# A hybrid streaming-encoder layer: packed token columns for the state-space inputs, moved memory rates, and another order at the end of the MLP's up-projection

## The chip, the cores and the metric

One core of a Trainium2 chip runs the whole program. The metric is the device time of one execution in microseconds (us), over several runs of the same program on the same chip.

## The reference

One residual layer over 1024 tokens of 1024 channels, in three sub-layers, each normalised before and after. All arrays are float32.

```python
def reference(x, mem, ...):
    h = rms_norm(x, norm_mix_pre)
    q, k, v, u, gate_logits = jnp.split(h @ w_in, splits, axis=-1)      # 512 columns each for q, k, v, u; 2048 for the gates
    gate_attn, gate_ssm = jnp.split(jax.nn.sigmoid(gate_logits + b_gate), 2, axis=-1)
    o_attn = stick_breaking_attention(q, k, v)                          # 8 heads of 64
    o_ssm = s5_branch(u, ...)                                           # 32 groups of 16 channels, 64 complex states each
    merged = gate_attn * (o_attn @ w_branch_attn) + gate_ssm * (o_ssm @ w_branch_ssm)
    x = x + rms_norm(merged @ w_out, norm_mix_post)
    h = rms_norm(x, norm_xa_pre)
    mem_n = rms_norm(mem, norm_mem)                                     # 256 memory rows
    x = x + rms_norm(memory_cross_attention(h, mem_n, ...), norm_xa_post)
    h = rms_norm(x, norm_ffn_pre)
    f = conv_ffn(h, w_up, conv_w, conv_b, w_down)
    return x + rms_norm(f, norm_ffn_post)

def conv_ffn(h, w_up, conv_w, conv_b, w_down):
    up = h @ w_up                                # 1024 -> 2 * 2816
    up = conv1d(up, conv_w, causal, width 3, per channel) + conv_b
    gate, val = jnp.split(up, 2, axis=-1)
    return (jax.nn.gelu(gate) * val) @ w_down    # 2816 -> 1024
```

## The kernel before

**Numbers in two halves.** Each float32 operand of a matmul is split into a high part (a copy into the type fp32r) and a low part (the difference), and each product is three matmuls: high by high, high by low, low by high (`mm3`, L148 to L151, of which the last three lines are the matmuls). The high parts are mostly made by ScalarE and the low parts by VectorE.

**The first part: input projection.** `hT` holds x transposed, in four tiles: high and low part of channel blocks 0 to 3 and of 4 to 7; in each, the 1024 tokens lie side by side. A step `tokens(now, n, i, k)` is the three matmuls of one block of 128 channels for one tile of 128 tokens, the tokens as weights and 512 columns of the projection streaming. For n = 0 the result is the attention's V, and the tile is 128 consecutive tokens. For n = 1 it is u, the state-space branch's input; tile i holds the tokens i, i+8, i+16 and so on (`slice(i, S, 8)`), since the scan that follows works with eight interleaved streams. After the eighth step of a tile ScalarE evicts it: V into `vr` and on to DRAM, scaled by each token's rate (L447), u into `U`, scaled by `r8` (L444). The normalisation is thus applied behind the projection. `r8` holds the rates in the interleaved order: they are written to DRAM (`rx_d`, L413) and read back (L414) on SP's queue of DMAs. Squares of x (for the rates) come from x loaded as rows, in a ring of two buffers named `xr` (pool `p0`).

The raw float32 weights of the projection arrive in a ring of four buffers named `wr`; w_high (L393, ScalarE) and w_low (L397, VectorE) make the pairs `wh`/`wl` (`wx` for the last pair). The same ring takes the 256 memory rows later (`mem_load`), whose rates `mem_rate` makes: a Square on ScalarE, a scaled sum on VectorE, a power on POOL.

All of this is ordered by hand. `at(t, go)` puts a step into a heap at a planned time t, and the steps are issued in the order of these times; a step of TensorE is planned at 0.70 (`STEP`), and `line(t, ...)` places a list of steps at and after t. PE, ACT, DVE and POOL keep that order (a manual schedule), and so does SP's queue. While the u tiles run, VectorE builds the state-space tables (L660 and around, with two tables' cosines on ScalarE), and 16 narrow matmuls (L694, `W` with `Y`) stand between u steps. The first gate job (`ps_f`, L149 to L151) follows the last u tile.

**The MLP's up-projection.** The pair of blocks p = 0 to 21 (`NF` = 22) is 128 gate channels and 128 value channels. A seven-product block scheme makes both for all 1024 tokens from 7 products of 12 matmuls instead of 8. `order` lists (pair, product); `prep` makes the weights' operand some products ahead; `product` issues the 12 matmuls and then drains the bank: a copy on ScalarE (L1927) where the bank is the first into its place in `uu`, an addition on VectorE (L1932) otherwise. Products of one pair share banks: 1, 6, 7 and 4 accumulate into one, 5 and 3 into another, 2 has its own. `chores` places the convolution of the pair before among the products: `c_scale` on ScalarE (L2023), two `c_tap` on VectorE (L2027) for each half (1 is the value half, `cv`; 0 the gate half, `cg`), then `c_gelu` and the gating product `c_mul` (L2035). The gated halves and their sums go to DRAM as `sd`; those of the weights as `td`.

**The down-projection** is a second seven-product scheme: `load2` reads an operand pair back as `raw`, `prep2` splits it into `dn` (L154 on ScalarE, L155 on VectorE), and `mm_step` issues 12 matmuls (L2177 to L2179) into four banks, four token tiles in turn. Its first products take the operands of pairs that were done long before; the last pair's are wanted by the eleventh step. The banks of the accumulators change hands at its door: a bank of the down-projection opens once the up-projection's product in it has been drained. In the MLP a scheduler orders ACT and DVE, from the order of the code and its own estimates.

**The tail.** The last product of the scheme goes token tile by token tile. ScalarE squares the finished half row (L2256), VectorE multiplies it by the gain (L2257), `rstd_of` makes the row's rate (L213, L214, and a power on POOL), and a scaled addition and a DMA end the row.

Of the kernel before, what the change touches and what calls it, by code (L numbers as in the profile page):

```python
# [45 lines left out]
def kernel(ctx: ExitStack, tc: tile.TileContext, a: dict, out: bass.AP, dbg=None):  # L46
# [382 lines left out]
    accs_ = {}  # L429

    def tokens(now, n, i, k):

        sl = slice(i * P, (i + 1) * P) if n == 0 else slice(i, S, 8)
# [4 lines left out]
        mm3(acc, h_hi(k, sl), h_lo(k, sl), wh, wl, k == 0, k == KT - 1)  # L438
# [60 lines left out]
    def mem_load(i):  # L499
        raw["m", i] = px.tile([P, 1024], F32, tag="wr", name="wr", bufs=4)  # L500
        dma(raw["m", i], a["mem"][i * P:(i + 1) * P, :])
# [10 lines left out]
    line(70.0, (lambda: mem_load(0), 0), (lambda: mem_load(1), 16.0), (lambda: mem_rate(0), 1.4), (lambda: mem_rate(1), 2.6),  # L512
# [307 lines left out]
    u_begin = clock  # L820
    for c in range(4):
        at(30.0 + c, lambda _, c=c: w_load(1, c))
        at(last_v + 1.3 + 1.4 * c, lambda _, c=c: w_high(1, c))
        at(last_v + 2.4 + 1.4 * c, lambda _, c=c: w_low(1, c))
# [977 lines left out]
    class Pair:  # L1802
# [46 lines left out]
        def operand(self, prod):  # L1849
# [12 lines left out]
            if prod == 5:  # L1862
                src = self.add("1", self.wv[:, lo_], self.wg[:, lo_])
            elif prod == 6:
                src = self.add("2", self.wv[:, hi_], self.t["1"])
# [15 lines left out]
    order[-7:] = [(NF - 1, 1), (NF - 2, 4)] + [(NF - 1, n) for n in (5, 6, 2, 7, 3, 4)]  # L1881
# [193 lines left out]
    def chores(w, r):  # L2075
# [10 lines left out]
        slot = r - 2 if p == 0 else r  # L2086
        if live and slot == 0:
            c_scale(p, 1)
        elif live and slot == 1:
            c_tap(p, 1, 1)  # L2090
        elif live and slot == 2:
            c_tap(p, 1, 2)
            c_scale(p, 0)
        elif live and slot == 3:
            c_tap(p, 0, 1)
        elif live and slot == 4:
            c_tap(p, 0, 2)
# [51 lines left out]
    for s in range(last + 1):  # L2149
# [6 lines left out]
        if s == 9:  # L2156
            down_load(0)
        chores(w, r)
        product(*order[s])
        if s >= last - 4:  # L2160
            for _ in range(3 if s == last - 4 else 1):
                load2()
        if s in (last - 3, last - 2):
            prep2()
# [16 lines left out]
    def out_row(i, t, ss, two):  # L2181
# [3 lines left out]
        rr = rstd_of(p8, ss, two=two)  # L2185
        yt = y[t // 4][:, i]
# [18 lines left out]
    for prod in (2, 1, 5, 6, 3, 7):  # L2205
        acc = bank_b if prod in (2, 5, 3) else bank_a
        for k in range(NF // 2):
# [11 lines left out]
            elif i2 == 4:  # L2219
                chores(NF + 1, 4)  # L2220
                r7.close()
# [23 lines left out]
    for i in range(4):  # L2245
# [11 lines left out]
        V.tensor_tensor(y[1][:, i, h0], bank_a[i], gfo[:, h0], op=ALU.mult)  # L2257
        out_row(i, 4 + i, ss1[i], True)
# [71 lines left out]
```

## Time and profile before

| what | before |
|---|---|
| runs | 1667.44, 1664.74, 1667.44 us; median 1667.44 |
| the profiled execution | 1663.46 us, its span 1661.7 us |
| granted TensorE clock | 0.997 |
| TensorE matmuls / weight loads | 1642.4 us (99%) / 1382.1 us (83%) |
| VectorE, ScalarE, POOL | 1163.4 us (70%), 881.7 us (53%), 199.3 us (12%) |
| HBM | 163 GB/s over the span |

The span is what the profiler saw from the first to the last instruction; the execution's own time is 1.8 us more. The span divides as follows on TensorE's timeline: V tiles to 54.24 us, u tiles from there to 104.23, then gates, attention, cross-attention, and the MLP, whose up-projection issues its last matmul at 1443.16 and whose down-projection begins at 1445.09.

A row of the timeline reads: start in us, duration in us, engine, line, operation, output<-inputs, shapes, and in brackets how long the engine had idled and for whom. Matmuls are pipelined, so that their starts are closer together than they are long: what counts is the distance of the starts. A group's row has the count, then busy time in us and the mean of one in ns, then the idle time before it and what ended it.

### The profile page before, as it was taken

The page shows a single profiled execution, that of the slowest core. Times are in us where ns is not written, and L with a number is a line of the kernel's source. Part 1 is how long each engine was busy: PE and PEld are TensorE (multiplying, and loading weights), DVE is VectorE, ACT ScalarE, POOL GpSimd, SP SyncE. Part 2 cuts the span into 40 slices and gives each one's busy share as a digit, 9 for nine tenths or more (in the row PEclk, how much of TensorE's full clock was granted, in tenths as well). Part 3 has the DMA queues.
Part 4 walks back from the last instruction along what each step waited for, and adds up shares of the span by engine and source line. Part 5 has one row for each costly group of instructions (what it writes and reads, how often), then busy time and mean ns, then how long its engine had stood idle before and what let it go on. Part 6 is the DMA issues. An engine that isn't in the chain of part 4 may idle for free.

```text
span 1661.7 us, 22448 instructions
## 1 busy us (share of the span) xinstructions
PE 1642.4 (99%) x8126; PEld 1382.1 (83%) x8126; DVE 1163.4 (70%) x1617; ACT 881.7 (53%) x1458; POOL 199.3 (12%) x233
## 2 busy tenths in 40 slices
PE   9999999999999999999999999999999999999998
PEld 7998888888888978888888888888888888788886
DVE  7778637676866678467655678888887788965473
ACT  5435346676766554345444556655565555654441
POOL 5000002233332000011000000111111111000010
PEclk9999999999999999999999999999999999999999
DMA  9412244232432964464313584677777676697672
GB/s 324 121 46 66 67 141 110 65 90 86 109 108 92 341 208 135 161 205 164 140 64 135 192 285 176 179 212 211 216 197 202 185 201 189 204 350 235 194 234 83
DMA packets 125438, 279.26 MB, mean 168 GB/s; under 512 B 23696, under 2 KB 28304, under 8 KB 125200
## 3 DMA queue, kind: packets, MB, share of 16 engines
q1 hardware_dynamic: 113664, 251.35, 46.0%
q0 software_dynamic: 9360, 18.09, 6.2%
q10 hardware_dynamic: 2304, 8.39, 1.3%
q8 instruction: 64, 1.05, 0.3%
q14 instruction: 46, 0.38, 0.1%
HBM read 203.98 MB, written 67.38 MB: 163 GB/s over the span
## 4 chain that ended last, share of the span: by engine, by line
PE 90%; DVE 5%; DMA 2%; ACT 1%; issue 1%; SPq 0%; DVEq 0%; POOL 0%; POOLq 0%; ACTq 0%
PE ps_p L1916 8%; PE ps_p L1914 8%; PE ps_p L1915 8%; PE ps_f L149 7%; PE ps_f L151 6%; PE ps_f L150 6%; PE ps_d L2177 4%; PE ps_d L2178 4%; PE ps_d L2179 4%; PE ps_m L149 3%; PE ps_m L151 3%; PE ps_m L150 3%; PE ps_o L1065 2%; PE ps_w L1040 2%; PE ps_z L149 1%; PE ps_z L151 1%
## 5 line engine op out<-in xcount | busy, mean ns | idle before, releaser
L149 PE MATMUL ps_f<-hT,wh 128*128 128x512 f32 x384 | 165.4, 431 | 0.0
L151 PE MATMUL ps_f<-hT,wl 128*128 128x512 f32 x384 | 150.9, 393 | 0.0
L150 PE MATMUL ps_f<-hT,wh 128*128 128x512 f32 x384 | 150.6, 392 | 0.0
L1915 PE MATMUL ps_p<-qS,bm 128*128 128x512 f32 (+2 forms) x368 | 141.3, 384 | 1.7 <-DVE qS L1741 1.7
L1914 PE MATMUL ps_p<-qS,bm 128*128 128x512 f32 (+2 forms) x368 | 141.3, 384 | 0.6 <-DVE uu L1932 0.6
L1916 PE MATMUL ps_p<-qS,bm 128*128 128x512 f32 (+2 forms) x368 | 141.4, 384 | 0.0
L155 DVE TENSOR_TENSOR dn<-raw,dn 128x1024 fp32r<-128x1024 f32 x77 | 93.4, 1222 | 66.5 <-ACT dn L154 63.2
L1020 DVE TENSOR_TENSOR_SCAN s<-s,zcol 128x128 f32<-128x128 f32 (+3 forms) x96 | 99.4, 1037 | 50.5 <-ACT s L1015 49.9
L154 ACT CAST dn<-raw 128x1024 fp32r<-128x1024 f32 x77 | 80.6, 1054 | 92.1 <-PE ps_d L2179 38.7
L2177 PE MATMUL ps_d<-dn 128*128 128x512 f32 x308 | 119.9, 389 | 1.5 <-ACT uu L1927 1.5
L1026 POOL TENSOR_TENSOR s<-s,s 128x127 f32<-128x127 f32 (+4 forms) x96 | 89.3, 931 | 256.1 <-DVE s L1020 222.3
L2179 PE MATMUL ps_d<-dn 128*128 128x512 f32 x308 | 119.8, 389 | 0.0
L2178 PE MATMUL ps_d<-dn 128*128 128x512 f32 x308 | 119.8, 389 | 0.0
L1916 PE MATMUL ps_p<-qA,bm 128*128 128x512 f32 (+2 forms) x272 | 105.0, 386 | 0.5 <-DVE bm L1847 0.5
L1914 PE MATMUL ps_p<-qA,bm 128*128 128x512 f32 (+2 forms) x272 | 105.1, 386 | 0.0
L1915 PE MATMUL ps_p<-qA,bm 128*128 128x512 f32 (+2 forms) x272 | 105.0, 386 | 0.0
L1927 ACT COPY uu<-ps_p 128x512 f32<-128x512 f32 (+2 forms) x90 | 51.5, 572 | 83.8 <-PE ps_p L1916 83.8
L1859 POOL DMA_DIRECT2D bm<-in_ffn_up_T x61 | 52.8, 866 | 354.4 <-ACT bm L1858 161.0
L1015 ACT ACTIVATE s<-ps_z,rates_x 128x128 f32<-128x128 f32 (+3 forms) x96 | 56.3, 587 | 57.7 <-PE ps_z L1007 29.1
L151 PEld LDWEIGHTS ps_f<-hT,wl 128*128 128x128 f32 x384 | 72.1, 188 | 16.1
L1915 PEld LDWEIGHTS ps_p<-qS,bm 128*128 128x128 f32 x368 | 70.1, 190 | 15.1 <-DVE qS L1741 2.0
L1914 PEld LDWEIGHTS ps_p<-qS,bm 128*128 128x128 f32 x368 | 70.0, 190 | 14.2 <-issue 1.2
(545 smaller groups left out, 4446.6 us busy)
## 6 DMA issues: line engine op xcount, KB each, us to landing
raw<-sd SPq DMA_DIRECT2D x77, 256.0 KB, 3.3
bm<-in_ffn_up_T POOLq DMA_DIRECT2D x61, 256.0 KB, 5.5
ws<-in_w_in_T SPq DMA_DIRECT2D x24, 512.0 KB, 3.3
ws<-in_xa_wo_N SPq DMA_DIRECT2D x23, 512.0 KB, 4.1
wv<-in_ffn_up_T SPq DMA_DIRECT2D x22, 512.0 KB, 4.3
wg<-in_ffn_up_T SPq DMA_DIRECT2D x22, 512.0 KB, 4.1
dr<-in_ffn_down SPq DMA_DIRECT2D x22, 512.0 KB, 6.7
td<-st SPq DMA_DIRECT2D x44, 256.0 KB, 6.4
```

The costliest lines, as they stand in the source:

```text
L149: T.matmul(acc, sh, mh, start=first, stop=False)
L150: T.matmul(acc, sh, ml, start=False, stop=False)
L151: T.matmul(acc, sl, mh, start=False, stop=last)
L155: (lo or V).tensor_tensor(dl, src, f(dh), op=ALU.subtract)
L1020: V.tensor_tensor_scan(s2[:, n0:n1][:, ::-1], s2[:, n0:n1][:, ::-1], zcol.to_broadcast([P, n1 - n0]), 1.0 if diag else s2[:, n1:n1 + 1], o ...
L1026: G.tensor_tensor(s1[:, n0:e], s1[:, n0:e], s2[:, n0 + 1:e + 1], op=ALU.mult)
L1914: T.matmul(acc, bm[:, 0, ks], q[:, 0, k, cs], start=alone and k == 0, stop=False, skip_group_check=True)
L1915: T.matmul(acc, bm[:, 0, ks], q[:, 1, k, cs], start=False, stop=False, skip_group_check=True)
L1916: T.matmul(acc, bm[:, 1, ks], q[:, 0, k, cs], start=False, stop=k == 3, skip_group_check=True)
L2177: T.matmul(acc[i], v[:, 0, 0, sl], v[:, 0, 1], start=first, stop=False, skip_group_check=True)
L2178: T.matmul(acc[i], v[:, 0, 0, sl], v[:, 1, 1], start=False, stop=False, skip_group_check=True)
L2179: T.matmul(acc[i], v[:, 1, 0, sl], v[:, 0, 1], start=False, stop=last, skip_group_check=True)
```

## The change

**Packed columns for u.** For each of the eight u tiles, four new copies on ScalarE (`every_eighth`) put the tile's tokens side by side: from each tile of `hT` the columns i, i+8 and so on of four channel blocks, 128x512 at a time, into a buffer `uc`. The two `uc` of a tile (high and low) stand in the ring `wr` of four. The u steps then take their weights from `uc`. The copies are planned 4.2 ahead of their tile and 1.1 apart; those of the first tile 1.3 ahead and 0.6 apart.

**Memory rows and rates.** Since `wr` now holds `uc`, the two memory rows' tiles go into `xr`, the ring of the rows of x. Their loads and rates move from the planned time 70.0 to 47.5.

**End of the up-projection.** The last pair's products come in the order 6, 5, 7, 2, 4, 3 instead of 5, 6, 2, 7, 3, 4, with the operand code to suit. The last pair's gate half is convolved before its value half. In the last five steps the product now stands ahead of the chores, and the first two `prep2` one step later. From the fifth step from the end to the fifth step of the down-projection ScalarE keeps the order of the code (`seam`).

**Tail.** The gain of the last four rows is handed to `out_row` and issued behind the call of `rstd_of`.

```diff
+    def every_eighth(i, j, kk):
+        if kk == 0:
+            ucol.setdefault(i, []).append(px.tile([P, 1024], F32R, tag="wr", name="uc", bufs=4))
+        C.copy(ucol[i][j][:, kk * 512:(kk + 1) * 512].rearrange("p (k t) -> p k t", k=4), hT[j][kk][:, :, i::8])
     def tokens(now, n, i, k):
-        sl = slice(i * P, (i + 1) * P) if n == 0 else slice(i, S, 8)
+        sl = slice(i * P, (i + 1) * P)
...
-        mm3(acc, h_hi(k, sl), h_lo(k, sl), wh, wl, k == 0, k == KT - 1)
+        stat = [c[:, k * P:(k + 1) * P] for c in ucol[i]] if n else (h_hi(k, sl), h_lo(k, sl))
+        mm3(acc, *stat, wh, wl, k == 0, k == KT - 1)
...
     def mem_load(i):
-        raw["m", i] = px.tile([P, 1024], F32, tag="wr", name="wr", bufs=4)
+        raw["m", i] = p0.tile([P, D], F32, tag="xr", name="xr", bufs=2)
...
-    line(70.0, (lambda: mem_load(0), 0), (lambda: mem_load(1), 16.0), (lambda: mem_rate(0), 1.4), (lambda: mem_rate(1), 2.6),
+    line(47.5, (lambda: mem_load(0), 0), (lambda: mem_load(1), 14.0), (lambda: mem_rate(0), 1.4), (lambda: mem_rate(1), 2.6),
...
+    for i in range(8):
+        for n, (j, kk) in enumerate(((0, 0), (1, 0), (0, 1), (1, 1))):
+            t_ = u_begin + 8 * STEP * i - 4.2 + 1.1 * n if i else u_begin - 1.3 + 0.6 * n
+            at(t_, lambda _, i=i, j=j, kk=kk: every_eighth(i, j, kk))
...
-    order[-7:] = [(NF - 1, 1), (NF - 2, 4)] + [(NF - 1, n) for n in (5, 6, 2, 7, 3, 4)]
+    order[-7:] = [(NF - 1, 1), (NF - 2, 4)] + [(NF - 1, n) for n in (6, 5, 7, 2, 4, 3)]
...
+        one = int(p < NF - 1)
         if live and slot == 0:
-            c_scale(p, 1)
+            c_scale(p, one)
...
-        chores(w, r)
+        if s < last - 4:
+            chores(w, r)
+            product(*order[s])
+            continue
+        if s == last - 4:
+            seam = ExitStack()
+            seam.enter_context(tc.manual_schedule(engines={mybir.EngineType.Activation}))
         product(*order[s])
-        if s >= last - 4:
-            for _ in range(3 if s == last - 4 else 1):
-                load2()
-        if s in (last - 3, last - 2):
+        chores(w, r)
+        for _ in range(3 if s == last - 4 else 1):
+            load2()
+        if s in (last - 2, last - 1):
             prep2()
...
             elif i2 == 4:
                 chores(NF + 1, 4)
+                seam.close()
...
-        V.tensor_tensor(y[1][:, i, h0], bank_a[i], gfo[:, h0], op=ALU.mult)
-        out_row(i, 4 + i, ss1[i], True)
+        out_row(i, 4 + i, ss1[i], True,
+                lambda: V.tensor_tensor(y[1][:, i, h0], bank_a[i], gfo[:, h0], op=ALU.mult))
```

How the instructions stand on an engine's own queue, at three places. In these rows a line number is that of the kernel named; behind the name is the operation, output<-inputs and the shape.

**ScalarE, from the last weights of the projection on.** `wr` are raw weights, `wh` and `wx` their high parts, `vr` evictions of V, `U` of u, `uc` the packed columns, `mss` the memory rows' sums of squares. Before:

```order
L393 CAST wh_646<-wr_478 128x1024
L393 CAST wx_656<-wr_489 128x1024
L447 ACTIVATE vr_667<-ps_m_554,zcol_109,rates_x_119 128x512
L444 ACTIVATE U_148<-ps_m_659,zcol_109,r8_153 128x32x16
L447 ACTIVATE vr_701<-ps_m_605,zcol_109,rates_x_119 128x512
L444 ACTIVATE U_148<-ps_m_688,zcol_109,r8_153 128x32x16
```

Changed:

```order
L435 COPY uc_680<-hT01_127 128x512
L435 COPY uc_688<-hT11_129 128x512
L451 ACTIVATE U_148<-ps_m_668,zcol_109,r8_153 128x32x16
L435 COPY uc_717<-hT00_126 128x512
L454 ACTIVATE vr_719<-ps_m_605,zcol_109,rates_x_119 128x512
L435 COPY uc_733<-hT10_128 128x512
L512 ACTIVATE xr_616,mss_738<-xr_616 128x1024
L435 COPY uc_717<-hT01_127 128x512
L435 COPY uc_733<-hT11_129 128x512
L512 ACTIVATE xr_618,mss_764<-xr_618 128x1024
```

The copies stand ahead of the casts `wx` and between the evictions, and the two memory Squares now stand there too.

**SP's queue of DMAs, around the rates of x.** `rx_d` as an output is the write of the rates, `r8` their load back, `ws` weights for later stages, `v_d` V on its way to DRAM, `row_k` another reader of the rates, `wr<-in_mem` and `xr<-in_mem` the memory rows. Before:

```order
L259 DMA ws_916<-in_w_in_T 128x1024
L259 DMA ws_964<-in_w_in_T 128x1024
L413 DMA rx_d_122<-rates_x_119 128x8x1
L448 DMA v_d_66<-vr_622 128x512
L414 DMA r8_153<-rx_d_122 128x8
L287 DMA row_k_121<-rx_d_122 128x512
L501 DMA wr_784<-in_mem 128x1024
L501 DMA wr_786<-in_mem 128x1024
```

Changed:

```order
L508 DMA xr_616<-in_mem 128x1024
L508 DMA xr_618<-in_mem 128x1024
L413 DMA rx_d_122<-rates_x_119 128x8x1
L259 DMA ws_964<-in_w_in_T 128x1024
L455 DMA v_d_66<-vr_626 128x512
L414 DMA r8_153<-rx_d_122 128x8
L287 DMA row_k_121<-rx_d_122 128x512
L259 DMA ws_1012<-in_w_in_T 128x1024
```

The memory loads moved from behind the load of `r8` to just ahead of the write of the rates, in the place of a load of later weights (`ws`).

**ScalarE at the end of the up-projection.** `uu<-ps_p` is the drain of a product, `cv` and `cg` the convolution's scales of the value and gate half, `dn` the casts for the down-projection. Before:

```order
L154 CAST dn_13051<-raw_13034 128x1024
L2023 ACTIVATE cv_13013<-uu_9482,cw_9746 128x1024
L1927 COPY uu_9482<-ps_p_12870 128x4x128
L154 CAST dn_13051<-raw_13055 128x1024
L2023 ACTIVATE cg_13067<-uu_9482,cw_9746 128x1024
```

Changed:

```order
L1940 COPY uu_9530<-ps_p_12918 128x4x128
L154 CAST dn_13041<-raw_12991 128x1024
L2036 ACTIVATE cg_13076<-uu_9530,cw_9794 128x1024
L154 CAST dn_13099<-raw_12994 128x1024
L154 CAST dn_13099<-raw_13020 128x1024
L2036 ACTIVATE cv_13117<-uu_9530,cw_9794 128x1024
```

The last drain that is ScalarE's (product 4, now the last but one) stands ahead of the convolution's first scale, which is now that of the gate half.

More of the change, by code (lines that the diff above doesn't have):

```diff
@@ L427, in x_low @@
         V.tensor_tensor(dl, xt[t][:, 4 * kk:4 * kk + 4], f(dh), op=ALU.subtract)
-    accs_ = {}
+    accs_, ucol = {}, {}
+    def every_eighth(i, j, kk):
+        if kk == 0:
+            ucol.setdefault(i, []).append(px.tile([P, 1024], F32R, tag="wr", name="uc", bufs=4))
+        C.copy(ucol[i][j][:, kk * 512:(kk + 1) * 512].rearrange("p (k t) -> p k t", k=4), hT[j][kk][:, :, i::8])
     def tokens(now, n, i, k):
-        sl = slice(i * P, (i + 1) * P) if n == 0 else slice(i, S, 8)
+        sl = slice(i * P, (i + 1) * P)
         if k == 0:
@@ L1862, in operand @@
             if prod == 5:
-                src = self.add("1", self.wv[:, lo_], self.wg[:, lo_])
+                src = self.t["1"] if "1" in self.t else self.add("1", self.wv[:, lo_], self.wg[:, lo_])
             elif prod == 6:
+                if "1" not in self.t:
+                    self.add("1", self.wv[:, lo_], self.wg[:, lo_])
                 src = self.add("2", self.wv[:, hi_], self.t["1"])
@@ L2086, in chores @@
         slot = r - 2 if p == 0 else r
+        one = int(p < NF - 1)
         if live and slot == 0:
-            c_scale(p, 1)
+            c_scale(p, one)
         elif live and slot == 1:
-            c_tap(p, 1, 1)
+            c_tap(p, one, 1)
         elif live and slot == 2:
-            c_tap(p, 1, 2)
-            c_scale(p, 0)
+            c_tap(p, one, 2)
+            c_scale(p, 1 - one)
         elif live and slot == 3:
-            c_tap(p, 0, 1)
+            c_tap(p, 1 - one, 1)
         elif live and slot == 4:
-            c_tap(p, 0, 2)
+            c_tap(p, 1 - one, 2)
         if live and p and slot == 5:
@@ L2157 @@
             down_load(0)
-        chores(w, r)
-        product(*order[s])
-        if s >= last - 4:
-            for _ in range(3 if s == last - 4 else 1):
-                load2()
-        if s in (last - 3, last - 2):
+        if s < last - 4:
[5 more added lines that the diff above has]
+            seam.enter_context(tc.manual_schedule(engines={mybir.EngineType.Activation}))
+        product(*order[s])
+        chores(w, r)
+        for _ in range(3 if s == last - 4 else 1):
+            load2()
+        if s in (last - 2, last - 1):
             prep2()
@@ L2179, in mm_step, with out_row @@
             T.matmul(acc[i], v[:, 1, 0, sl], v[:, 0, 1], start=False, stop=last, skip_group_check=True)
-    def out_row(i, t, ss, two):
+    def out_row(i, t, ss, two, gain=lambda: None):
         xt = p8.tile([P, D], F32, tag="x2t", name="x2t", bufs=3)
@@ L2185, in out_row @@
         rr = rstd_of(p8, ss, two=two)
+        gain()
         yt = y[t // 4][:, i]
```

## The prediction

> **What bounds the kernel now.** I read the page first, then TensorE's waits, then the timelines of the places that the diff touches.
>
> ```profile
> PE 1642.4 (99%) x8126; PEld 1382.1 (83%) x8126; DVE 1163.4 (70%) x1617; ACT 881.7 (53%) x1458; POOL 199.3 (12%) x233
> PE 90%; DVE 5%; DMA 2%; ACT 1%; issue 1%; SPq 0%; DVEq 0%; POOL 0%; POOLq 0%; ACTq 0%
> ...
> PE ps_d L2177 <- ACT uu L1927: 1.5, 1, 1.5
> ```
>
> TensorE is busy for 99% of the span and is 90% of the chain that ended last. Time can only be won by matmuls that follow each other faster, or by one of TensorE's few waits going away. The third line is the longest wait that the diff touches: at the door of the down-projection.
>
> ```profile
> 43.18 0.39 PE L149 MATMUL ps_m<-wh,hT 128*128 128x512 f32 x1
> ...
> 54.24 0.41 PE L149 MATMUL ps_m<-wh,hT 128*128 128x512 f32 x1
> ...
> 76.94 1.85 PE L694 MATMUL ps_m<-Y,W 128*128 128x16 f32 x16
> ...
> 104.23 0.39 PE L149 MATMUL ps_f<-hT,wh 128*128 128x512 f32 x1
> ...
> 106.95 0.49 PE L723 MATMUL ps_m<-ident,U 128*128 128x128 f32 x3
> ```
>
> These are starts on TensorE's timeline. 43.18 to 54.24 are the last two V tiles, 48 matmuls: 0.2304 us each. At 54.24 the u tiles begin; up to the small W matmuls at 76.94 they are 31 steps of 3, 93 matmuls: 0.2441 us each. At 104.23 the first gate job begins, 12 matmuls to 106.95: 0.2267 us each. Only the u tiles take every eighth column as weights, and their weight loads show it (groups of loads in 59 to 104 us, then in 7 to 59):
>
> ```profile
> L150 PEld LDWEIGHTS ps_m<-wl,hT 128*128 128x128 f32 x42 | 13.9, 331 | 0.0
> ...
> L150 PEld LDWEIGHTS ps_m<-wl,hT 128*128 128x128 f32 x54 | 11.0, 203 | 2.7 <-DVE wl L467 0.5
> ```
>
> A load of 331 ns no longer fits under a matmul of 0.23 us.
>
> **Part 1, packed weights.** 64 steps of 3 are 192 matmuls. They gain 192 x (0.2441 - 0.2304) = 2.6 us by their neighbours before, 192 x (0.2441 - 0.2267) = 3.3 us by those after; I take 3.0.
>
> What it costs is 32 copies of 128x512 on ScalarE, four ahead of each u tile. No row has ScalarE reading every eighth float, so the bounds come from these:
>
> ```profile
> L423 ACT CAST hT<-xt 128x512 fp32r<-128x512 f32 x16 | 9.6, 616 | 15.4 <-DVE xt L420 15.4
> L793 ACT COPY U<-ps_m 128x512 f32<-128x512 f32 x8 | 8.9, 1222 | 3.6 <-PE ps_m L791 3.6
> ...
> L596 DVE TENSOR_TENSOR t<-sp x1: 189/189/189, 43.8 to 43.8; 128x32 f32<-128x32 f32 x1
> ...
> L600 DVE TENSOR_TENSOR t<-pi,sp x1: 203/203/203, 44.6 to 44.6; 128x32 f32<-128x32 f32 x1
> ```
>
> Below: 0.62 us, a cast between packed tiles. Above: 1.22 us, L793, which writes every eighth float. Between: L600 reads one operand at 36 bytes' distance (pi[:, :, 1]) and takes 14 ns longer for 32 elements than L596, 0.44 ns an element, over 512 elements 0.22 us. I take 0.62 + 0.22 = 0.84 us, since L600 is a strided read by an elementwise engine, as the copy is; both ends are kept. On ScalarE an instruction starts about 0.1 us before the one ahead ends, so a copy adds 0.74 us to its queue.
>
> The Trainium skill (page "SBUF — State Buffer", section "Door 1: The DMA port swizzle") speaks against the copies: it says SBUF is read in lines of 16 bytes and that every access which crosses to a new line pays, so four floats is the widest free stride. At eight floats each element is a new line, which would put the copies near the upper row and the sum at that of the first rival below; the weight loads (331 against 203 ns) agree with it, L600 only by a third.
>
> **The first u tile waits.** The copies' buffers are the four that hold the raw weights of this projection, so a copy waits until VectorE has made the low part of a weight.
>
> ```profile
> 51.69 2.17 ACT L393 CAST wh<-wr 128x1024 fp32r<-128x1024 f32 x2
> 54.44 1.05 ACT L393 CAST wx<-wr 128x1024 fp32r<-128x1024 f32 x1 [0.58 <-PE ps_m L151]
> ...
> 52.74 3.49 DVE L397 TENSOR_TENSOR wl<-wr,wh 128x1024 fp32r<-128x1024 f32 x3
> ```
>
> The three low parts end at about 53.9, 55.1 and 56.2. High columns, first half: 53.9 to 54.75, so the first matmul comes at 54.8 and not at 54.24 (0.55 late). Low columns: 55.1 to 55.95, so the third matmul comes at 56.0 and not at 55.25 (0.75 late). The cast wx and the second halves then end near 58.3, when step 4 begins. Cost 1.3 us. With 0.62 us copies it would be 0.95.
>
> **The rates for U.** ScalarE's eviction of u tile 0 needs r, that is the write of the rates to DRAM and a load back. What was idle time until then now stands in front of copies.
>
> ```profile
> 50.91 0.38 SPq L413 DMA_DIRECT2D rx_d<-rates_x  x1
> 62.01 0.32 SPq L414 DMA_DIRECT2D r<-rx_d  x1
> ...
> 63.71 0.78 ACT L444 ACTIVATE U<-ps_m,zcol,r 128x512 f32<-128x512 f32 x1 [7.54 <-DMA r<-rx_d]
> 64.39 0.77 ACT L447 ACTIVATE vr<-ps_m,zcol,rates_x 128x512 f32<-128x512 f32 x1
> ...
> wr<-in_mem SPq DMA_DIRECT2D x2, 512.0 KB, 6.6
> ...
> 48.00:49.00 1.00, 1.00 (x6) 0.81 (x5) 0.46 (x1) 1.00 (x3) 0.00 (x0) 1.00 0.98 393
> ```
>
> If r lands as before, ScalarE does U at 63.71, then by its order a copy, vr, a copy: 0.68 + 0.74 + 0.68 + 0.84 ends at 66.65. TensorE is at tile 2 at 54.24 + 1.3 + 16 x 0.69 = 66.6, and the third matmul wants that second copy half a us later. So it fits, with 0.4 us to spare. But the second memory load now waits for the last Square of x (near 48.8) and is issued just ahead of the write of the rates, in SP's queue. Bounds: no delay, if the write is slow for its many short pieces alone; 48.8 + 6.6 - 50.9 = 4.5 us, if it waits until the load has landed. I take 512 KB at the 393 GB/s of the window quoted, 1.3 us, since that is what the load needs of the DMA engines.
>
> VectorE feels the same. It now has a memory rate ahead of the first table, and waits there for ScalarE's Square:
>
> ```profile
> 60.20 2.38 DVE L660 TENSOR_TENSOR x<-x,turns 128x8 f32<-128x8 f32 x7
> ...
> 67.74 0.69 DVE L678 TENSOR_TENSOR W<-W,tq 128x512 f32<-128x512 f32 x1
> ...
> 88.92 1.58 POOL L507 TENSOR_TENSOR rates_m<-mr,mhalf 128x1 f32<-128x1 f32 x2 [14.95 <-DVE mr L506]
> ```
>
> Square near 66.6 to 67.8, the rate and its power on POOL (1.58 / 2 = 0.8) and the memset to 68.8, tables and W 60.20 to 68.43 = 8.2 us, so W at 77.0. TensorE comes to the W matmuls at 54.24 + 1.3 + 31 x 0.69 = 76.9. Both cases pass a late r on, and not twice: 1.3 us late less what is spare, 1.0 us. VectorE is 8 us behind by then; its row at 74.00 waited 5.57 us for the next table's buffer, and it idles 6.15 us before 100.83, so this is not carried further.
>
> ```profile
> 74.00 2.38 DVE L660 TENSOR_TENSOR x<-x,turns 128x8 f32<-128x8 f32 x7 [5.57 <-POOL x L657]
> ...
> 100.83 1.23 DVE L267 TENSOR_TENSOR wl<-ws,wh 128x1024 fp32r<-128x1024 f32 x1 [6.15 <-ACT wh L263]
> ```
>
> **Part 2, the end of the up-projection.**
>
> ```profile
> 1443.16 0.39 PE L1916 MATMUL ps_p<-qA,bm 128*128 128x512 f32 x1
> 1445.09 0.50 PE L2177 MATMUL ps_d<-dn 128*128 128x512 f32 x1 [1.53 <-ACT uu L1927]
> 1445.42 0.39 PE L2178 MATMUL ps_d<-dn 128*128 128x512 f32 x1
> ...
> 1443.32 1.24 ACT L2023 ACTIVATE cv<-uu,cw 128x1024 f32<-128x1024 f32 x1 [0.21 <-DVE uu L1932]
> 1444.47 0.56 ACT L1927 COPY uu<-ps_p 128x512 f32<-128x512 f32 x1
> ...
> 1453.05 1.22 DVE L2035 TENSOR_TENSOR cg<-cg,cv 128x1024 f32<-128x1024 f32 x1
> ...
> 1459.97 1.05 ACT L154 CAST dn<-raw 128x1024 fp32r<-128x1024 f32 x1 [6.95 <-DMA raw<-sd]
> ```
>
> Now the last product's copy stands behind a convolution scale on ScalarE. The gap of 1.93 us is 1.70 too long, and the first matmul's pitch of 0.33 adds 0.1: 1.8 us. In the new order the last product but one (4) is copied near 1440.9 to 1441.45, before TensorE is at the door, and the last (3) is added on VectorE. What is late next is that add: it stands behind a tap that needs ScalarE's new scale. 1441.45 + 1.0 (a cast) + 1.25 (the scale) = 1443.6, tap 1.3, add 0.7: 1445.6. Only the fourth down tile has that bank, at 1443.4 + 9 x 0.227 = 1445.4. So 0.2 to 0.3 us of waiting stays: gain 1.5. Bounds: 1.8 with no wait, 0 if the add comes 1.5 us later.
>
> The last pair's gating product (L2035) then falls from 1453 to about 1459.5, since casts are now ahead of it. From its end to the end of the cast that needs its DRAM round trip it took 1461.0 - 1454.3 = 6.7 us, and the low part 1.3 more: 1467.5, for a matmul at 1443.7 + 10 x 2.72 = 1470.9. Hidden, with 3.4 us left.
>
> **Part 3, the tail.**
>
> ```profile
> 1655.64 0.69 DVE L2257 TENSOR_TENSOR y<-ps_d,g_ffn_post 128x512 f32<-128x512 f32 x1 [4.53 <-ACT jk L2256]
> 1656.25 0.15 DVE L213 TENSOR_TENSOR rstd<-ss 128x1 f32<-128x1 f32 x1
> 1656.44 0.15 DVE L214 TENSOR_SCALAR rstd<-rstd 128x1 f32<-128x1 f32 x1
> ```
>
> By the order, the gain now stands between L213 and L214 and not after both. L213 starts at 1655.64, the gain 0.1 later, L214 at about 1656.35: 0.1 us won.
>
> **Sum.** -3.0 + 1.3 + 1.0 - 1.5 - 0.1 = -2.3 us. The profiled execution, 1663.46 (span 1661.7), goes to 1661.2. That execution was 4 us under the median of the runs, 1667.44, so I put the difference on the median: 1665.1.
>
> **Rivals.**
> 1. ScalarE becomes the bound of the u tiles (slower). At L793's 1.22 us a copy adds 1.12 to the queue: 35.8 us. With wx, two vr, seven U, two Squares, two tables' three functions, two E and the gate job's cast at their timeline spacing, 17 more: 52.8 us from 54.0, 106.8, and VectorE's low part (1.23) makes 108.1 where that matmul, the third after 104.23, was at 104.7. U loses 3.4, parts 2 and 3 give 1.6: 1669.2. It decides from copies of about 1.1 us. For: the weight loads and L793. Against: L600.
> 2. The copies cost 0.62 and r is on time: -3.0 + 0.95 - 1.6, 1663.8. For: L793 may be slow for its writing, and r's 11 us are not bandwidth. Against: the load issued ahead.
> 3. The door does not open earlier, the add being late on VectorE: -0.8 in all, 1666.6.
>
> **Chances.** Forecast (0.7 to 1.0 us copies) 0.45, rival 1 0.20, rival 2 0.27, rival 3 0.08. 0.2% (3.3 us) is about what a measurement of this kernel can tell: faster is below 1664.1, slower above 1670.8. Faster: over half of rival 2 and a third of the forecast, 0.32. Slower: half of rival 1 (r late as well) and a little more, 0.13. Same 0.55. Range 1660.8 to 1670.8: rival 2 with all of part 1's 3.3 and a spread of the runs as shown at the low end, rival 1 with r late at the high end.
>
> **What would show it.** Copies: the duration of the new ScalarE group. Packing: weight loads near 200 ns and a pitch near 0.23 in the u tiles. First tile: waits of its first and third matmul near 0.6 each. r: its issue near 63. Door: the first down matmul 0.3 us behind the last up matmul, the fourth tile's waiting for VectorE. I am wrong if ScalarE runs without idle time through the u tiles, or if the cast on the gating product's round trip waits past 1470.

## The result, and the profile after

| | before | changed |
|---|---|---|
| median of 16 runs each | 1665.74 us | 1668.81 us |
| lowest and highest | 1661.99, 1668.59 | 1667.62, 1673.25 |
| ratio, 95% interval | | 1.0022 [1.0016, 1.0028] |
| profiled execution, span | 1663.46, 1661.7 | 1667.62, 1665.5 |

The change made the kernel slower by 2.7 to 4.7 us. TensorE's timeline of the changed kernel shows where (start, duration, line; in brackets the idle time before it and for whom):

```profile
47.98 0.39 PE L149 MATMUL ps_m<-wh,hT 128*128 128x512 f32 x1
...
54.49 0.50 PE L149 MATMUL ps_m<-wh,uc 128*128 128x512 f32 x1 [0.82 <-ACT uc L435]
...
62.14 0.39 PE L149 MATMUL ps_m<-wh,uc 128*128 128x512 f32 x1
...
66.80 0.40 PE L151 MATMUL ps_m<-wx,uc 128*128 128x512 f32 x1
...
97.36 0.50 PE L151 MATMUL ps_m<-wh,uc 128*128 128x512 f32 x1 [1.73 <-ACT uc L435]
...
109.08 0.40 PE L149 MATMUL ps_f<-hT,wh 128*128 128x512 f32 x1
...
1448.88 0.39 PE L1929 MATMUL ps_p<-qS,bm 128*128 128x512 f32 x1
1449.11 0.39 PE L2197 MATMUL ps_d<-dn 128*128 128x512 f32 x1
...
1658.32 0.39 PE L2199 MATMUL ps_d<-dn 128*128 128x512 f32 x1
```

Before, the last V tile began at 48.71, the gate job at 104.23:

```profile
48.71 0.39 PE L149 MATMUL ps_m<-wh,hT 128*128 128x512 f32 x1
...
1654.44 0.39 PE L2179 MATMUL ps_d<-dn 128*128 128x512 f32 x1
```

With these starts the 3.8 us between the spans divide as follows. The stretch from the start of the last V tile to the gate job is taken as one, since the copies' first wait falls at the border between V and u tiles; I call it the u stretch.

| stretch | before | changed | difference |
|---|---|---|---|
| to the last V tile | 48.71 | 47.98 | -0.73 |
| u stretch | 55.52 | 61.10 | +5.58 |
| gate job to the last up-projection matmul | 1338.93 | 1339.80 | +0.87 |
| door | 1.93 | 0.23 | -1.70 |
| down-projection | 209.35 | 209.21 | -0.14 |
| last matmul to the end | 7.26 | 7.18 | -0.08 |

The first and the third row are no part of the change: the third was 1338.7 to 1342.3 in seven profiles of kernels that have the instructions of before there. The views that follow say why the u stretch grew. First the busy time of each engine from 54.2 to 104.2 us (TensorE, weight loads, VectorE, ScalarE, POOL, each with its count; then the granted clock, the DMA share and GB/s), before:

```profile
54.20:104.20 50.00, 50.00 (x217) 49.80 (x217) 34.76 (x60) 17.91 (x23) 2.72 (x7) 1.00 0.18 44
```

and changed:

```profile
54.20:104.20 50.00, 45.37 (x196) 33.87 (x197) 32.97 (x59) 48.51 (x51) 2.63 (x6) 1.00 0.15 43
```

The copies' durations (minimum, median, maximum in ns) and a group of weight loads that read them (busy time, mean in ns):

```profile
L435 ACT CAST uc<-hT x32: 1104/1212/1257, 53.3 to 103.5; 128x512 fp32r<-128x512 f32 x32
```

```profile
L150 PEld LDWEIGHTS ps_m<-wl,uc 128*128 128x128 f32 x45 | 8.5, 188 | 1.9
```

TensorE's waits for the copies (us in total, times, longest):

```profile
PE ps_m L151 <- ACT uc L435: 3.6, 5, 1.7
...
PE ps_m L149 <- ACT uc L435: 1.3, 3, 0.8
```

And ScalarE's only idle time from 50 to 107 us, on its timeline:

```profile
65.48 0.78 ACT L451 ACTIVATE U<-ps_m,zcol,r 128x512 f32<-128x512 f32 x1 [1.49 <-DMA r<-rx_d]
```

ScalarE went from 17.9 to 48.5 us of work in 50. A copy takes 1.21 us (median), not 0.84. TensorE waits 4.9 us for copies; where ScalarE stood still, it waited 1.49 us for r. The packing itself does what it should: loads of 188 ns in place of 331, and 20 matmuls from 62.14 to 66.80 are 0.233 us apart in place of 0.2441.

### The profile page after: what moved, and what is told of

Its sections match the earlier page's. It is cut to its first block, busy times and chain, and to the rows that moved or that the text cites. A ratio compares the mean times of both kernels' runs of the same rounds, so it can differ in the third digit from the quotient of the medians.

```text
span 1665.5 us, 22489 instructions
## 1 busy us (share of the span) xinstructions
PE 1642.3 (99%) x8126; PEld 1369.9 (82%) x8126; DVE 1162.5 (70%) x1617; ACT 916.2 (55%) x1490; POOL 199.4 (12%) x233
## 4 chain that ended last, share of the span: by engine, by line
PE 87%; DVE 4%; ACT 3%; issue 1%; DMA 1%; DVEq 0%; POOL 0%; POOLq 0%; SPq 0%; ACTq 0%
PE ps_p L1927 8%; PE ps_p L1929 8%; PE ps_p L1928 8%; PE ps_f L149 7%; PE ps_f L151 7%; PE ps_f L150 6%; PE ps_d L2199 4%; PE ps_d L2198 4%; PE ps_d L2197 4%; PE ps_o L1076 2%; PE ps_w L1051 2%; PE ps_m L151 2%; PE ps_m L149 2%; PE ps_m L150 2%; PE ps_z L149 1%; PE ps_z L151 1%
## 5 line engine op out<-in xcount | busy, mean ns | idle before, releaser
L1870 POOL DMA_DIRECT2D bm<-in_ffn_up_T x61 | 52.8, 865 | 357.7 <-ACT bm L1869 194.9
```

## The experiments

Each kernel's ratio is against the kernel before on the same chip. "MLP's part" is the new end of the up-projection with the tail.

**The two halves of the change.** `u_only` has only the packed columns and the memory rows' move, `mlp_only` only the MLP's part.

> The packed columns and the moved memory rows alone; the end of the up-projection and the tail are as before. Theory A (ScalarE's queue bounds the u tiles, since a copy takes 1.21 us): the u tiles end 4.9 us later, as in the changed kernel, and nothing is given back, so 4 to 5 us slower than before (ratio 1.0025 to 1.0030), with TensorE waiting some 5 us for uc. Rival B (part of the loss sits behind the u tiles, in the MLP's new order): no more than 3 us slower, as the changed kernel is.

> The end of the up-projection and the tail alone; u tiles and memory rows as before. Theory A: the door's wait of 1.5 us and 0.1 us in the tail are won and nothing is lost, 1.9 us faster (ratio 0.9989), first down matmul 0.23 us behind the last up matmul. Rival B: the new order costs about as much ahead of the door as it wins there (between the gate jobs and the door the changed kernel lost 0.8 us), so within 0.5 us of before.

Measured: `u_only` 1673.08 us, ratio 1.0046 [1.0032, 1.0059], 5.3 to 9.8 us slower; `mlp_only` 1661.85, 0.9980 [0.9971, 0.9989], 1.8 to 4.8 us faster. So the MLP's part wins and the u part loses all. Both medians moved further than either theory said, though theory A's 1.9 us for `mlp_only` lies within its interval. The trace of `u_only` has a u stretch of 61.56 us, 6.0 more than before, a door of 2.22, and something new behind the door. Its timeline there:

```profile
1450.81 0.39 PE L1927 MATMUL ps_p<-qA,bm 128*128 128x512 f32 x1
1453.03 0.50 PE L2188 MATMUL ps_d<-dn 128*128 128x512 f32 x1 [1.84 <-ACT uu L1938]
1453.37 0.45 PE L2189 MATMUL ps_d<-dn 128*128 128x512 f32 x1
1453.62 0.63 PE L2190 MATMUL ps_d<-dn 128*128 128x512 f32 x1
1454.05 0.63 PE L2188 MATMUL ps_d<-dn 128*128 128x512 f32 x1
```

and the busy times of the next 4 us, with the granted clock behind POOL's:

```profile
1453.00:1457.00 4.00, 3.97 (x10) 3.12 (x11) 3.96 (x4) 3.95 (x4) 0.00 (x0) 0.57 0.52 196
```

Eight matmuls are 0.43 us apart at a clock of 0.57, and the down-projection takes 210.94 us, 1.6 more than before. Stretch, door and clock make 6.0 + 0.3 + 1.6 = 7.9 us. That the median's difference is 7.8 is luck in part: the span of this one execution is 9.5 us longer, and the other 1.6 lie in rows that the change does not touch. For `mlp_only` it shows a door of 0.23, 2.0 us with the down-projection and the tail, within the interval but 1.4 under its middle.

**What makes a copy slow.** `contig` reads 128 tokens side by side; `strides` gives each u tile another distance (code shortened; `dst` is the slice of `uc`):

```diff
-        C.copy(dst, hT[j][kk][:, :, i::8])
+        C.copy(dst, hT[j][kk][:, :, i * P:(i + 1) * P])              # contig
+        g = 8 if i > 4 else (4, 1, 2, 3, 4)[i]                       # strides
+        (V.tensor_copy if i == 6 else C.copy)(dst, hT[j][kk][:, :, i:i + (P - 1) * g + 1:g])
```

> The changed kernel with one thing altered: the copies read 128 tokens that lie side by side instead of every eighth, so u is made of the wrong tokens, and the work is otherwise the same. Theory A (the strided read is what makes a copy 1.21 us): copies of 0.62 us, waits for uc only at the first u tile (about 1 us), the gate job near 103.4, about 3 us faster than before and 6 faster than the changed kernel. Rival C (the copies are slow for what they write, or for contention with weight loads): copies over 1.0 us and the gate job still behind 107.

> The changed kernel with other sources for the copies, so u is made of wrong tokens: u tiles 0 to 4 take every 4th, every 1st, 2nd, 3rd and 4th token, tiles 5 and 7 every 8th, and tile 6 every 8th on VectorE. Theory A1 (a read costs more only beyond four floats' distance): 0.62 us for 1 to 4, 1.21 for 8. Rival A2 (the cost grows with the distance): 0.70, 0.79, 0.87 and 1.21 us. On VectorE: 1.2 us if it is the reading of memory that is slow, about 0.9 by the 0.44 ns an element that the prediction took from a strided operand there.

Measured: `contig` 1663.26, ratio 0.9992 [0.9983, 1.0001], u stretch 55.30 us. The copies' durations in `contig`:

```profile
L435 ACT CAST uc<-hT x32: 603/616/625, 53.3 to 93.5; 128x512 fp32r<-128x512 f32 x32
```

its busy times in the u tiles:

```profile
54.20:104.20 50.00, 48.94 (x220) 38.99 (x220) 34.17 (x60) 34.42 (x55) 2.79 (x8) 1.00 0.20 53
```

and the copies' durations in `strides`, for tiles 1 to 4 (distances 1, 2, 3, 4) and for VectorE at 8:

```profile
L441 ACT CAST uc<-hT x4: 618/632/632, 59.4 to 61.0; 128x512 fp32r<-128x512 f32 x4
...
L441 ACT CAST uc<-hT x4: 642/647/674, 66.4 to 69.7; 128x512 fp32r<-128x512 f32 x4
...
L441 ACT CAST uc<-hT x4: 901/931/947, 72.0 to 74.4; 128x512 fp32r<-128x512 f32 x4
...
L441 ACT CAST uc<-hT x2: 1112/1122/1131, 76.8 to 78.8; 128x512 fp32r<-128x512 f32 x2
...
L439 DVE CAST uc<-hT x4: 687/704/706, 91.4 to 93.2; 128x512 fp32r<-128x512 f32 x4
```

It is the read, and on ScalarE: 0.63, 0.65, 0.93, 1.12 us at 1 to 4 floats' distance and 1.21 at 8. Neither A1 nor A2 holds: two floats are nearly free, the price rises to four and is nearly flat behind. VectorE does the copy at 8 in 0.70 us, close to ScalarE's packed 0.63. The rule of the Trainium skill that the prediction weighed (page "SBUF — State Buffer", section "Door 1: The DMA port swizzle": lines of 16 bytes, four floats the widest free stride) is borne out at 8 on ScalarE, and not at 4, where the read is dear already. VectorE shows no sign of it: its packed rows of that size with two operands took 0.69 us (L678 in the prediction). A packed copy on VectorE was not run.

But `contig` was not the 3 us faster that theory A gave. With ScalarE free for 15 us and the matmuls 0.011 us closer, its u stretch is only 0.2 us shorter than before. So a full ScalarE is not the whole loss. The first u matmul still comes 5.95 us behind the last V tile's start in place of 5.53, TensorE waits another 0.9 us for copies' low columns, at tile 0 and at tile 2, and r is late.

**Fewer or other copies.** `hi_only` packs only the high columns; `mix` leaves tile 0 unpacked, gives VectorE the low columns, and puts the memory rates off to 24 us behind the start of the u tiles (parts of the edits):

```diff
+        for n, (j, kk) in enumerate(((0, 0), (0, 1))):                             # hi_only
+        (V.tensor_copy if j else C.copy)(dst, hT[j][kk][:, :, i::8])               # mix
+    for i in range(1, 8):                                                          # mix
+            t_ = u_begin + 8 * STEP * i - (6.2 if i == 2 else 4.2) + 1.1 * n       # mix
```

> The changed kernel with only the high columns packed (16 copies on ScalarE), the low ones read at every eighth column. Theory A: ScalarE has 36 us of work in 50, the waits for uc go except at the first tile (0.6 us). Three loads take 188 + 188 + 331 = 707 ns for three matmuls of 0.70 us, so the distance falls to 0.237 us and 192 matmuls win 1.5 us: about 1661. Rival E (one slow load in three holds TensorE as three did): distance 0.244, nothing won in the u tiles, 1662.5.

> The changed kernel with the copies put elsewhere: u tile 0 reads every eighth column as before, tiles 1 to 7 have their high columns packed by ScalarE (14 copies at 1.12 us of its queue) and their low ones by VectorE (14 at 0.6), tile 2's are asked for 2.0 earlier in the plan, and the memory rates' sums and powers come 24 us behind the start of the u tiles. Theory A (the price is ScalarE's time for a strided read): ScalarE's 17.9 us of work in the u tiles become 34 of 50 and VectorE's 34.8 become 43, none is full, TensorE no longer waits for uc, and 168 matmuls come 0.011 us sooner: 1.8 us ahead of the kernel with the MLP's part alone, about 1660. Rival D (the rates r, late by 1.8 us, hold the first U and the copies behind it, and W is late on VectorE): waits of 1 to 2 us come back, and it is no faster than the MLP's part alone, 1662.

Measured: `hi_only` 1662.04, 0.9985 [0.9976, 0.9994], u stretch 55.86, matmuls 0.236 us apart, so theory A's distance came, yet the stretch is 0.3 longer than before. `mix` 1661.57, 0.9979 [0.9970, 0.9988], u stretch 55.21. Both have ScalarE at 34 us of 50, and neither is measurably ahead of `mlp_only` (0.9980): rival D for `mix`, and for `hi_only` a gain that two waits for copies took back, 0.8 us at tile 0 and 1.0 at tile 2, behind the late r.

**The late r.** `mem_only` moves the memory rows and does nothing else.

> The kernel before with only the memory rows moved to the buffers of x's rows and to the planned time 47.5. Theory (the late r is the weight load of 512 KB that now stands between the write of the rates and their load back): r lands some 3.5 to 4 us after its issue instead of 1.6, ScalarE's first U starts near 65.5 instead of 63.7, and TensorE does not feel it, gate job near 104.2, time as before. Rival (r is late because of the copies): r lands after 1.6 us.

Its DMA issues from 45 to 70 us (times issued, KB, median us to landing):

```profile
ws<-in_w_in_T SPq DMA_DIRECT2D x2, 512.0 KB, 9.1
...
rx_d<-rates_x SPq DMA_DIRECT2D x1, 4.0 KB, 11.7
r<-rx_d SPq DMA_DIRECT2D x1, 4.0 KB, 3.4
```

and ScalarE's first U:

```profile
65.69 0.78 ACT L444 ACTIVATE U<-ps_m,zcol,r 128x512 f32<-128x512 f32 x1 [9.81 <-DMA r<-rx_d]
```

r lands 3.4 us after its issue (before 1.6), without any copy in the program, and TensorE does not feel it: u stretch 55.53. In all kernels with the rows moved to 47.5 r took 3.4 to 4.3 us by SP's queue, in those without 1.5 to 1.7. The moved rows took the place of a weight load ahead of the write of the rates; that load, 512 KB, now stands between write and read. On SP's queue in the changed kernel:

```profile
50.18 0.38 SPq L413 DMA_DIRECT2D rx_d<-rates_x  x1
50.61 0.57 SPq L259 DMA_DIRECT2D ws<-in_w_in_T  x1
...
61.91 0.33 SPq L414 DMA_DIRECT2D r<-rx_d  x1
```

The traffic of the changed kernel from 45 to 70 us, in 40 slices of 0.625 us, shows the load crawl until the write lands: 271 KB in the 7.5 us from 54.4 to 61.9 (31 KB in the kernel before, which has no load there). The rest of it begins to move at 403 GB/s at 61.9, just as r is issued:

```profile
GB/s 295 347 236 102 26 13 105 288 387 73 5 0 0 0 0 46 59 20 39 13 33 13 26 20 33 39 92 403 333 227 118 82 243 275 351 252 177 72 321 102
```

`mem_only` timed:

> The memory rows' move alone, timed. In three of three looks at kernels with it and the old end of the up-projection, ScalarE's cast ahead of the last drain waited 2.4 to 2.6 us for a load of raw, the door took 2.2 to 3.2 us and the clock fell behind it; in three of three looks at the kernel before, the door took 1.9 to 2.0 at full clock. Theory F1 (the move shifts that load for good): 2 to 3 us slower than before. Rival F2 (chance, in the kernel before too): the same as before within its interval.

Measured: 1665.25, ratio 1.0007 [0.9997, 1.0016]. So r late costs nothing alone. What it costs beside copies was asked in both directions. `after_r` and `mix_r` read r back by POOL's queue; `after_m` and `mix_m` put the memory rows into the ring of the later weights, so that SP's queue has no weight load there (parts of the edits):

```diff
-        dma(r8, rx_d.rearrange("t (q r) -> (t q) r", r=8))
+        at(57.0, lambda _: G.dma_start(r8, rx_d.rearrange("t (q r) -> (t q) r", r=8)))     # after_r, mix_r
-        raw["m", i] = p0.tile([P, D], F32, tag="xr", name="xr", bufs=2)
+        raw["m", i] = wpool.tile([P, 1024], F32, tag="ws", name="mw", bufs=WS)             # after_m, mix_m
-    line(47.5, ...
+    line(70.0, ...                                                                         # after_m, mix_m
```

> The changed kernel with one edit: the rates r are read back through POOL's queue of DMAs, so that they no longer stand behind the weight load of 512 KB on SP's. Theory (ScalarE's queue is full, so the 1.5 us in which it waits for r count once in the u tiles): r lands near 63.7, ScalarE no longer waits for it, the gate job comes near 107.6 in place of 109.1, and the kernel is 1.5 us faster than the changed one, 1667.3. Rival (the wait for r is hidden, since TensorE waits for copies that are late anyway): gate job at 109, no gain. Mishap that is possible: POOL's way is slower than SP's, r lands later and more is lost.

> The kernel with high columns packed by ScalarE and low ones by VectorE, with r read back through POOL's queue. Its two waits behind U (1.13 us for tile 3's columns, 0.87 for tile 6's) came where ScalarE had been held until r landed at 65.5. Theory: the first of them goes, gate job near 102.6 in place of 103.4, 0.8 us faster, about 1660.8. Rival: no change.

> The changed kernel with the memory rows in the ring of the later weights (ws) in place of xr, at the old planned time 70: then no weight load stands between the write of the rates and their load back, and r comes on SP's queue as before. POOL's queue was the wrong way to test it: r landed 1.95 us later still, and the u tiles grew by 1.8. Theory (the u tiles follow r one to one, since ScalarE's queue is full): r lands 1.6 us behind its issue, near 63.5, ScalarE waits no more for it, u tiles 1.5 us shorter (53.1 in place of 54.6), 1667.3 against 1668.8 for the changed kernel. Rival: the u tiles follow r only when it comes later than the copies ahead of U end (64.0), and other copies are late anyway: no shorter than 54.3.

> High columns packed by ScalarE and low ones by VectorE, tile 0 unpacked, memory rows in the ring of the later weights at the old planned time. Theory: with r near 63.5 the wait of 1.13 us for tile 3's columns goes, the u tiles take 48.2 us in place of 49.2 (50.0 before) and the kernel stands 0.5 to 1 us ahead of the MLP's part alone, 0.9976 of before. Rival: another wait takes its place, 49.2.

| kernel | r lands after its issue | first U | u stretch | time | ratio |
|---|---|---|---|---|---|
| changed | 3.5 | 65.48 | 61.10 | 1668.81 | 1.0022 [1.0016, 1.0028] |
| `after_r` | 5.8 | 67.43 | 62.92 | 1670.26 | 1.0043 [1.0029, 1.0057] |
| `after_m` | 1.6 | 63.88 | 58.61 | 1672.07 | 1.0042 [1.0027, 1.0058] |
| `mix` | 3.7 | 65.38 | 55.21 | 1661.57 | 0.9979 [0.9970, 0.9988] |
| `mix_r` | 5.9 | 67.19 | 57.68 | 1664.72 | 1.0005 [0.9996, 1.0014] |
| `mix_m` | 1.7 | 62.35 | 53.19 | 1659.36 | 0.9966 [0.9954, 0.9979] |

POOL's way was slower than SP's, the mishap named beforehand. In both families a first U 1.8 to 1.95 us later cost 1.8 (`after_r`) and 2.5 us (`mix_r`), and r on time gave 2.5 and 2.0 back. Neither number is r's alone: in `after_r` the granted clock fell to 0.50 from 70.25 to 77.08 behind a wait of 2.10 us for a copy, and in the two `_m` kernels the memory rows' Squares also come 20 to 27 us later on ScalarE (and `mix_m` does not put off the memory rates as `mix` does). `after_m` loses more than its gain at once: the memory rows hold the ring of weights until ScalarE, full, squares them at 95.84, and a cast of the gate jobs waits for its weights (ScalarE's timeline):

```profile
95.84 1.05 ACT L512 ACTIVATE mw<-mw 128x1024 f32<-128x1024 f32 x1
...
111.95 1.05 ACT L263 CAST wh<-ws 128x1024 fp32r<-128x1024 f32 x1 [4.42 <-DMA ws<-in_w_in_T]
```

In `mix_m` no such wait is left, and TensorE runs through. The u stretch's start and end on its timeline:

```profile
47.97 0.39 PE L149 MATMUL ps_m<-wh,hT 128*128 128x512 f32 x1
...
101.16 0.40 PE L149 MATMUL ps_f<-hT,wh 128*128 128x512 f32 x1
```

and the busy times from 54.2 to 104.2:

```profile
sum 50.00, PE 50.00 PEld 41.68 DVE 43.66 ACT 34.89 POOL 2.76; mean PE 50.00 PEld 41.68 DVE 43.66 ACT 34.89 POOL 2.76
```

`mix_m` is 3.5 to 7.7 us faster than before, faster than both kernels of this case. Its lead over `mlp_only` (0.9980) lies within the intervals.

**The door.** `noseam` is `mlp_only` without the stated order on ScalarE; `door3` is the kernel before with the last drain's copy made three times.

> The MLP's part and the tail alone, but without the stated order on ScalarE: the scheduler orders it. The prediction took the new order of the products for the cause of the door's gain: then the first down matmul follows the last up matmul within 0.3 us. If the stated order is what opens it, a wait of about 1.5 us for a copy of uu stays.

> The kernel before with ScalarE's copy of the last up-projection product made three times in place of once, so that the down-projection's first bank opens 0.96 us later: an idle time of 2.9 us. Theory F (an idle time of some 2 us at the door makes the granted clock fall to about half for 3 us, as in the profile of the packed columns alone, and costs another 1.6 us): distances of 0.43 us behind the door and 2.6 us slower than before. Rival G (the low clock there was a disturbance of that one execution): full clock, 1.0 us slower.

`noseam` keeps a wait for ScalarE's copy; the new order of the products alone won 0.4 of the 1.7 us:

```profile
1446.26 0.39 PE L1918 MATMUL ps_p<-qS,bm 128*128 128x512 f32 x1
1447.78 0.50 PE L2185 MATMUL ps_d<-dn 128*128 128x512 f32 x1 [1.14 <-ACT uu L1929]
```

`door3` (1669.89, ratio 1.0027 [1.0016, 1.0037]) got more than it asked for, since the scheduler put casts between the three copies: a door of 5.38 us, then a clock of 0.50 and a down-projection of 211.80 us, 2.45 longer. So it shows that a widened door brings the low clock, but not from which width on. The kernel before and the packed columns were profiled again:

> The kernel before, looked at again. Open is why the MLP's part won 3.4 us where the two profiles show 2.0 (1.7 at the door, 0.2 in the pitch and the tail). Theory F: the idle time at the door varies from execution to execution (1.9 us in the first profile, 2.2 in that of the packed columns alone, both with the same order on every engine), and where it passes some 2 us the clock falls to about 0.57 for 4 us: then a look at the kernel before shows it too, at about 1.6 us. Rival H: the door is as in the first profile, 1.9 us at full clock, and the difference lies in waits elsewhere.

> The same as the look before it, a third one: by theory F one of the two has a low clock behind the door; by rival H none.

> The packed columns and moved memory rows alone, looked at again. It lost 7.8 us, of which its first profile shows 4.9 in the u tiles and 1.6 in the low clock behind the door. Theory F: the u tiles again 4.7 to 5.0 longer than before, and the low clock only if the door's idle time is again above 2 us. Rival H: the rest lies in other waits, which this look shows again at the same places.

| kernel | door, start to start | down-projection | u stretch |
|---|---|---|---|
| `noseam` | 1.52 | 209.36 | 55.51 |
| before; `before_b`; `before_c` | 1.93; 1.99; 1.98 | 209.35; 209.36; 209.36 | 55.52; 55.52; 55.82 |
| `mem_only_t` | 1.98 | 209.35 | 55.51 |
| `u_only` | 2.22 | 210.94 | 61.56 |
| `mem_only` | 3.04 | 210.70 | 55.53 |
| `u_only_b` | 3.16 | 210.99 | 60.12 |
| `door3` | 5.38 | 211.80 | 55.51 |

At the door the clock stays up to 1.99 us; from 2.22 it falls to half, for 3.4 us and in `door3` for 6.8, at a price of 1.3 to 2.5 us. This is no threshold for TensorE as a whole. All 19 profiles have a shorter wait in the up-projection, 1.8 us from start to start, and half clock sets in during it or within 2 us behind it. In the kernel before (the wait, then the busy times behind it with a granted clock of 0.51):

```profile
1032.00 0.29 PE L1914 MATMUL ps_p<-qS,bm 128*128 128x128 f32 x1
1033.81 0.33 PE L1915 MATMUL ps_p<-qS,bm 128*128 128x128 f32 x1 [1.52 <-DVE qS L1741]
...
1034.20:1041.10 6.90, 6.90 (x29) 6.33 (x29) 6.83 (x12) 3.68 (x9) 0.20 (x1) 0.51 0.42 152
```

There the half clock lasted 3.4, 6.8 or 10.2 us, differently from execution to execution of one program: 6.8 in the first profile of before, 10.2 in `before_b`. The 3.4 us between these two can cost 1.7 us, half of what their stretches from gate job to door differ by (1338.93 and 1342.32). So a part of the spread of all these times arises there, and the same length of wait does not bring the same clock.

What widens the door is a load: in `mem_only` the cast ahead of the last drain waited for it.

```profile
1443.38 1.04 ACT L154 CAST dn<-raw 128x1024 fp32r<-128x1024 f32 x1 [2.40 <-DMA raw<-in_ffn_down]
1444.33 1.24 ACT L2023 ACTIVATE cv<-uu,cw 128x1024 f32<-128x1024 f32 x1
1445.47 0.56 ACT L1927 COPY uu<-ps_p 128x512 f32<-128x512 f32 x1
```

That the memory rows' move shifts this load for good (F1) is not borne out: the same program, timed, had a door of 1.98 and the time of before. Rival F2 stands, chance from execution to execution. That the clock of the kernel before falls at its door in a share of the executions would explain the 1.4 us by which `mlp_only`'s runs beat its trace; none of its three profiled executions shows it, so this stays open.

## Why the prediction was wrong

It forecast 2.3 us faster at 0.45, and 3.1 us slower (by the medians) came. The time lay inside the range, and the bound was rival 1's, which had 0.20. That the range held is luck in part: it was counted from the median of three runs, 1667.44, where 16 runs give 1665.74, and as a difference it ended at +3.4. Of the prediction's two signs of being wrong the first came: ScalarE had only 1.49 us of idle time in the u tiles.

- **The copies: the step that failed.** 0.84 us was taken between 0.62 and 1.22 "since L600 is a strided read by an elementwise engine". L600 is VectorE's. On ScalarE the copy took 1.21, the upper bound to 0.01, on VectorE 0.70. The nearest row was of the right access and the wrong engine; L793, ScalarE's own at eight floats' distance, was kept for the upper bound alone because it writes at that distance instead of reading. `contig` confirms the step: with packed reads and nothing else altered the copies took 0.62 us and the u stretch fell from 61.10 to 55.30.
- **ScalarE as the bound.** Rival 1's point of decision (1.1 us) and its sum were right: 52.8 us of work forecast from 54.0, and 52.5 done from 53.25 to 107.26, where the gate job's cast ends. Its path was not: the low part behind that cast was ready at 108.52, and the third matmul of the gate job, at 109.54, did not wait for it. TensorE had lost its time before, waiting for copies within the u tiles (the last time at 97.36). The rival put that matmul 3.4 us later, and left r's delay to the edge of the range; it came 4.8 later (109.54 for 104.7). The 1.49 us in which ScalarE stood still for r are of the size of the difference, which does not show that they are its cause. `contig` shows that even with cheap copies the packing, as placed, won 0.2 us.
- **The packing: -3.0 taken, -2.1 measured.** 192 x (0.2441 - 0.233). The u tiles' matmuls did not come down to the neighbours' mean of 0.2286, though their loads became shorter than the V tiles' (188 against 203 ns).
- **The first tile: +1.3 taken.** From the last V tile's start to the first u matmul it took 6.51 us in place of 5.53, 0.98 more (0.55 forecast), and from the second to the third matmul 0.80 in place of 0.23, 0.57 more (0.75 forecast): 1.55 in all, right in size.
- **r: +1.0 taken, 2 to 2.5 by the `_m` kernels, not r's alone.** That r would be late, and by 1.3 us, was right (1.8 for the first U). The cause named, a write held up by the memory load ahead of it, was wrong: r was issued on time (61.91, before 62.01) and landed late, because of the weight load which the memory load pushed behind the write. And the price was too small by these kernels, in which copies stand behind the first U.
- **The door: -1.5 taken, -1.70 and 0.14 in the down-projection measured.** The fourth tile did not wait: VectorE's add ended at 1451.18, practically when its matmul started (1451.15). By `noseam` the gain is mostly the stated order's on ScalarE. The gating product's round trip was hidden, as forecast: the cast behind it came at 1470.77, past the 1470 of the prediction's second sign, but the whole down-projection began 5.7 us later than forecast and none of its matmuls waited. The clock behind the door was not thought of.
- **The tail: -0.1 taken, -0.08 measured.**

## What to carry to other kernels

The price of an access belongs to the engine and the pattern together: before work is moved to an engine because it has idle time, look for a row of that engine with that distance, and where there is none, plan with the upper bound. A wait that an engine could afford (here ScalarE's 7.5 us for r) becomes a stall as soon as work is queued behind it, and moving one load changes what stands between another write and its read. An idle time of TensorE of about 2 us can cost more than itself, since the clock may fall behind it; look at the granted clock behind each such wait, as its length alone did not decide here.

## What the runs showed of the hardware

- ScalarE reading float32 from SBUF, 128x512: 0.63 us at distances of 1 and 0.65 at 2 floats, 0.93 at 3, 1.12 at 4, 1.21 at 8. VectorE at 8: 0.70 us.
- From start to start, TensorE's granted clock fell to half behind 2.22 us and more at the door and not behind 1.99 and less. Elsewhere it fell behind 1.8 us (up-projection, all 19 profiles) and 2.49 (`after_r`, 69.26), and stayed full behind 2.12 (changed kernel, 97.36) and 2.60 (`mix_r`, 69.70). The Trainium skill (page "TensorE: Matmul & The Clock Gate", section "Part 1: The HAM clock gate (the "warmup" mystery)") says that the clock falls to half after at least one idle window of about 3.4 us, a window that runs freely. The half clock agrees, and so do its lengths here, 3.4 us and two or three times that (the program's end aside); the idle time does not: half clock came with 1.8 us between starts.
- A write of 4 KB of single rates took 10.4 to 11.7 us to land in all kernels. Of the 512 KB load issued behind it on SP's queue only about half had moved by then in the changed kernel, at 13 to 92 GB/s, and the rest began at 403.
